# One decoder trunk, two ways to set the order of its instructions

## The chip, the cores and the metric

The kernel runs on 1 core of one Trainium2 chip. The metric is the device time of the program in microseconds; for the kernel before it is 1557.64 us, the median of 3 runs (1557.45 to 1557.89).

A core has five instruction streams that matter here: TensorE (PE, matmuls into eight PSUM banks), VectorE (DVE), ScalarE (ACT), GpSimd (POOL) and SyncE (SP), whose stream here only starts DMA transfers. Each works through its own queue in the order in which it was written, and waits on semaphores for the results of the others.

## The reference

Two decoder layers on 512 tokens of width 1024. Layer 0 mixes tokens by retention (4 heads), layer 1 by an mLSTM (4 heads); after each comes a causal ConvFFN of width 2816. Each of the four blocks is normed, modulated by columns computed from `c`, and added to the residual.

```python
c_act = silu(c)
for i in range(2):
    sh_t, sc_t, gt_t, sh_f, sc_f, gt_f = split(c_act @ ada_w[i] + ada_b[i], 6)
    h = rmsnorm(x, norm_tok_g[i]) * (1 + sc_t) + sh_t
    y = retention_mixer(h) if i == 0 else mlstm_mixer(h)
    x = x + gt_t * y
    h = rmsnorm(x, norm_ffn_g[i]) * (1 + sc_f) + sh_f
    u = causal_dwconv(h @ w_up[i], conv_w[i], conv_b[i])      # 3 taps
    a, b = split(u, 2)
    x = x + gt_f * ((silu(a) * b) @ w_down[i])
return rmsnorm(x, final_g)

# retention, per head, chunks of 128: q, k rotated by position (rope)
s = (q @ k.T) * decay;  y = groupnorm(s @ v + cross part) ;  out = (silu(g) * y) @ w_out
# mLSTM, per head: q, k through a 4-tap conv and silu; two gates give running weights
s = (q @ k.T) * w_intra;  h = (s @ v + ...) / max(|den|, exp(-m));  y = groupnorm(sigmoid(o) * h);  out = y @ w_out
```

## The kernel before, in words

**Layout and arithmetic.** Activations lie transposed, 128 channels on the partitions and 512 tokens along them; the residual `x` is eight tiles of 128x512. Products are in fp32r with both operands split into a high and a low part: `mm3` (L277 to L279) makes three matmuls, high by high, high by low, low by high. So each weight chunk of 0.5 MB (`Chunk`) is loaded into a `raw` buffer, ScalarE casts its high part (`high_part`, L160), and VectorE subtracts to get the low part (`low_part`, L165). `Pair.split` (L273, L274) does the same for activations.

**Stages.** `ret_start` norms the input and makes the first head's values and gates; then come the four retention heads (`heads`: q and k with `rope`, scores, values, gates, attend, group norm, output product), the norm into the ConvFFN (`Start`), the ConvFFN, the same for the mLSTM with its gates, the second ConvFFN, and the last norm with the stores (`End`). The recurrence over chunks is not computed step by step: each head covers all 512 tokens at once, in four strips of 128 keys.

Across a norm the work is cut in two halves of 256 tokens (`boundary`): the last output products run for half 0 and then for half 1, so that the first half's norm (squares L304 and L307, their sums L311, `root` L287 to L292, scaled tiles L328 and L331, high and low parts L337 and L339) runs beside the products of the second.

In a ConvFFN the products of most channel tiles run in a folded form (`folded`), 17 units of seven products with 256 columns (L418 to L420), two accumulating DMAs on GpSimd's queue and one of the down products per unit.

**What sets the order.** The program is a list of `items` (one or several weight chunks and a function that uses them). `Ahead` issues the load, the high part and the low part of a chunk up to four items before its use. In two places, `ret_start` and `folded.run`, the order of TensorE, VectorE, ScalarE and GpSimd is written out by hand: they stand in a `tc.manual_schedule` block, which keeps the program's order on these engines. Everywhere else the framework's own scheduler orders the instructions when the program is built, with the program's order as priority. Buffers come from pools: 55 slots of 128x512, six `raw`, eight high and eight low weight buffers, two `a` buffers, eight PSUM banks; a tile takes a free buffer of its pool.

**Modulation columns.** The columns of `c_act @ ada_w` are made one by one: a load of 0.5 MB and a VectorE multiply with accumulation (`gemv`, L140). 16 are made in `ret_start`. The other 80 wait in `side`: one or two go with each item until `LATER` = 32 are left; folded loop 0 takes eight of these (one in every second unit), and the items after it take the last 24.

The line numbers of the page are those of this kernel.

Of the kernel before, what the change touches and what calls it, by code (L numbers as in the profile page):

```python
# [29 lines left out]
LATER = 32  # L30
# [11 lines left out]
STRIPS = [(0, 512), (128, 384), (256, 256), (256, 256)]  # L42

# [25 lines left out]

@with_exitstack  # L70
def trunk(ctx: ExitStack, tc: tile.TileContext, xT, cb, pos, vec, ident, decay, zmask, ada, w_s0, w_in0, w_v0,
# [17 lines left out]

    def slot(s, dt=F32, w=T):  # L90
        return slots.tile([P, w], dt, tag="s", name=uid(s))

    def wide(s, dt=F32):
        if dt == F32:
            return raws.tile([P, D + 1], F32, tag="raw", name=s)
        return wpool.tile([P, WCOLS + WPAD], dt, tag=s[:3], name=s)

    def bank(s):
        return psum.tile([P, T], F32, tag="ps", name=uid(s))

    def aside(s):
        return asides.tile([P, D + 1], F32, tag="a", name=uid(s))

    V, A, G, PE = nc.vector, nc.scalar, nc.gpsimd, nc.tensor
# [3 lines left out]
    V.memset(const.tile([P, 32], F32, tag="pad", name="pad")[:], 0.0)  # L108
    ones = {}
    for name, v in (("d", 1.0 / D), ("v", 1.0 / DV), ("1", 1.0)):  # L110
        o = const.tile([P, P], F32R, tag=f"ones{name}", name=f"ones_{name}")
        V.memset(o[:].bitcast(F32), v)
        ones[name] = o
# [3 lines left out]
    nc.sync.dma_start(c_row[:1, :D], cb)  # L117
    x = [slot("x") for _ in range(KT)]
    for m in range(KT):
        nc.sync.dma_start(x[m][:], xT[m])  # L120
    c_ext = cond.tile([P, D + 1], F32, tag="c", name="c_ext")
    vecs = const.tile([P, NVEC], F32, tag="vec", name="vecs")
# [5 lines left out]
    eps_t = const.tile([P, 1], F32, tag="eps", name="eps_t")  # L128
    V.memset(eps_t[:], EPS)
    V.memset(const.tile([P, 40], F32, tag="pad2", name="pad2")[:], 0.0)  # L130
    V.memset(c_ext[:, D : D + 1], 1.0)

    mods = [const.tile([P, 48], F32, tag=f"mod{i}", name=f"mod_{i}") for i in range(2)]
    gains = [const.tile([P, 2 * KT], F32, tag=f"gain{i}", name=f"gain_{i}") for i in range(2)]

    def gemv(layer, f, raw=None):
        if raw is None:
            raw = aside("ada")[:]
            nc.sync.dma_start(raw, ada[layer, f])
        return V.scalar_tensor_tensor(raw, raw, 1.0, c_ext[:], op0=ALU.mult, op1=ALU.mult,  # L140
                                      accum_out=mods[layer][:, f : f + 1])

    def side_work(layer, f, after, raw=None):
        tc.keep_in_program_order(gemv(layer, f, raw))
        after()
# [22 lines left out]
    def low_part_added(w, hi, r, off=0):  # L168
# [3 lines left out]
        nc.gpsimd.dma_start(lo.bitcast(F32), w[:, r], accum_op=ALU.add)  # L172
        return lo

    class Chunk:
        def __init__(self, src, n, off):
            self.raw, self.r, self.off = wide(uid("raw")), slice(0, n), off
            nc.sync.dma_start(self.raw[:, self.r], src)
# [10 lines left out]
    class Beside(Chunk):  # L189
# [3 lines left out]
        def __init__(self, src):  # L193
            self.raw, self.r, self.off = aside("raw"), slice(0, WCOLS), 0
            nc.sync.dma_start(self.raw[:, :WCOLS], src)
# [13 lines left out]
    class Fold:  # L209
# [5 lines left out]
        def load(self):  # L215
            src = self.src
            self.a, self.b = wide(uid("wa")), wide(uid("wb"))
            nc.sync.dma_start(self.b[:, :WCOLS], src[1])
            nc.sync.dma_start(self.a[:, :WCOLS], src[0])
# [142 lines left out]
    class Ahead:  # L362


        def __init__(self):
            self.at = self.at_high = self.at_low = 0

        @property
        def flat(self):
            if not hasattr(self, "all"):  # L370
                self.all = [u for n, (uses, _, _) in enumerate(items) for u in uses if u.first == n]
            return self.all

        def may(self, n):
            u = self.flat[self.at]
            if any(n <= b < u.first for b in bars):
                return False
            return u.first <= n + AHEAD and (self.at < WBUFS or self.flat[self.at - WBUFS].last < n)

        def load(self):  # L380
            u = self.flat[self.at]
            u.chunk = Chunk(u.src, u.n, u.off)
            self.at += 1

        def high(self):
            self.flat[self.at_high].chunk.high()
            self.at_high += 1

        def low(self):
            self.flat[self.at_low].chunk.low()  # L390
            self.at_low += 1
    ahead = Ahead()

# [11 lines left out]
    def folded(folds, h, terms, pairs, downs, modulate):  # L405
# [4 lines left out]
        banks, sums, other = {}, {}, []  # L410
# [25 lines left out]
        def unit(i):  # L436
# [24 lines left out]
            else:  # L461
                ahead.high()
                ahead.high()
# [16 lines left out]
            else:  # L480
                ahead.low()
                ahead.low()
# [4 lines left out]
            if f:  # L487
                f.high_24()
                f.low_24(i % 2)
                if other:  # L490
                    layer, m, after, raw = other.pop()
                    gemv(layer, m, raw)
                    after()
            else:
                ahead.high()
                ahead.high()
# [13 lines left out]
            else:  # L510
                ahead.low()
                ahead.low()
# [5 lines left out]
            if modulate and side and i % 2 == 0 and i + 2 < len(folds):  # L518
                layer, m, after = side.pop(0)
                raw = aside("ada")[:]  # L520
                nc.sync.dma_start(raw, ada[layer, m])
                other.append((layer, m, after, raw))
            if i == len(folds) - 2:
                for _ in range(4):
                    ahead.load()
# [7 lines left out]
        def run(w):  # L533
            with tc.manual_schedule(engines={mybir.EngineType.PE, mybir.EngineType.DVE, mybir.EngineType.Activation,
                                             mybir.EngineType.Pool}):
                for i in range(len(folds)):
                    unit(i)
                last(len(folds) - 1)
                at = pairs[-1]
                c1, c2 = banks[len(folds) - 1]  # L540
                at.init(1, c2)
                at.init(0, c1)
                at.taps(1)
                at.taps(0)
                at.silu()
                at.gate()
                at.high()
                at.low()
        return first(), run

    def center_split(v, ps):

        t, m = slot("vt"), cols.tile([P, 1], F32, tag="vm", name=uid("vm"))
# [121 lines left out]
    class Start(Norm):  # L675
# [53 lines left out]
        def sums(self):  # L729
# [3 lines left out]
            d, xr = cols.tile([P, 4], F32, tag="dsh", name=uid("dsh")), self.xr  # L733
# [36 lines left out]
    class End(Norm):  # L770
# [7 lines left out]
        def use(self, p, k0, k1):  # L778
# [3 lines left out]
            for m in range(k0, k1):  # L782
# [3 lines left out]
                else:  # L786
                    tc.keep_in_program_order(
                        V.scalar_tensor_tensor(o[:, at : at + n], x[m][:, r], self.gain(m), self.rs[p][:, r],
                                               op0=ALU.mult, op1=ALU.mult))
            nc.sync.dma_start(out[k0:k1, :, r].rearrange("m p t -> p m t"),  # L790
# [120 lines left out]
    class Ffn:  # L911
# [77 lines left out]
        def items(self, norm):  # L989
# [4 lines left out]
            steps, run = folded(folds, self.h, self.start.terms, pairs, downs, self.layer == 0)  # L994
# [88 lines left out]
    def ret_scores(i):  # L1083
        st = R[i]
        tab = slot("tab")
        nc.sync.dma_start(tab[:], decay[i])
# [34 lines left out]
    def ret_start():  # L1121
# [16 lines left out]
        def load_ada(f, buf=None):  # L1138
            mod[f] = (buf or wide(uid("ada")))[:, : D + 1]
            nc.sync.dma_start(mod[f], ada[0, f])  # L1140

        def load_raw(k):
            raw[k] = wide(uid("raw"))
            nc.sync.dma_start(raw[k][:, :D], w_s0[k])
# [34 lines left out]
        with tc.manual_schedule(engines={mybir.EngineType.PE, mybir.EngineType.DVE, mybir.EngineType.Activation,  # L1179
# [386 lines left out]
```

## Time and profile before

| what | value |
|---|---|
| time, median of 3 runs | 1557.64 us |
| time of the profiled execution | 1559.0 us |
| its span, first to last instruction | 1557.2 us |
| mean granted TensorE clock | 0.993 |
| TensorE busy | 1519.7 us, 9037 matmuls |
| VectorE busy | 1194.2 us, 1832 instructions |
| ScalarE busy | 857.9 us, 1277 instructions |
| GpSimd busy | 205.4 us, 232 instructions |
| read from HBM | 193.13 MB |

A row of a group names the line, the engine, the operation, the tiles (written from read), the shape and the count, then busy us, the mean ns of one, and the idle time before them with what ended it. In a row of waits, the engine and its instruction stand before the arrow and what it waited for behind it. In a row of the timeline the first two numbers are the start and the duration in us; the bracket is the idle time ahead of it and what ended that. The end of a matmul is modelled, so matmuls overlap in the record.

### The profile page before, as it was taken

The numbers are of one execution on the slowest core, as the hardware profiler recorded it, in microseconds if no ns is written. First come the engines' busy times: TensorE is split into PE (matmuls) and PEld (weight loads), VectorE is DVE, ScalarE is ACT, GpSimd is POOL, SyncE is SP. The second block draws the span as 40 slices with busy tenths as digits, with TensorE's granted clock in tenths as the row PEclk, the third lists the DMA queues.
The fourth block names the chain that finished last, engine by engine and source line by source line (L and its number), as shares of the span: only waits on it lengthen the run. The fifth ranks groups of instructions, "written<-read, shape, count | busy, mean of one in ns | idle before, by whom it ended". The sixth has DMA issues, their size and how long they took to land.

```text
span 1557.2 us, 23255 instructions
## 1 busy us (share of the span) xinstructions
PE 1519.7 (98%) x9037; PEld 1344.6 (86%) x9037; DVE 1194.2 (77%) x1832; ACT 857.9 (55%) x1277; POOL 205.4 (13%) x232
## 2 busy tenths in 40 slices
PE   9999999999999999999999899999999999999997
PEld 7778888887988999999988778888889889999997
DVE  7985778686997888887776677776788977777775
ACT  4534524453456777676654444454545666777763
POOL 0121001110130111111100011001022201111102
PEclk9999999999999999999999999999999999999999
DMA  8833465545315888788434342443422258777751
GB/s 299 313 115 109 142 192 171 187 163 181 123 41 126 211 210 220 208 200 209 160 127 131 122 122 95 135 131 116 159 69 69 69 134 193 198 193 186 188 141 55
DMA packets 72369, 241.87 MB, mean 155 GB/s; under 512 B 9905, under 2 KB 12337, under 8 KB 72258
## 3 DMA queue, kind: packets, MB, share of 16 engines
q1 hardware_dynamic: 59874, 195.28, 37.8%
q0 software_dynamic: 12384, 45.09, 15.3%
q8 instruction: 71, 1.16, 0.3%
q14 instruction: 40, 0.33, 0.1%
HBM read 193.13 MB, written 2.12 MB: 125 GB/s over the span
## 4 chain that ended last, share of the span: by engine, by line
PE 75%; DVE 14%; issue 4%; ACT 3%; DMA 3%; POOL 1%; SPq 0%; DVEq 0%; ACTq 0%; POOLq 0%
PE p L418 7%; PE p L419 7%; PE p L420 7%; PE po L277 7%; PE po L278 7%; PE po L279 7%; PE pp L277 6%; PE pp L278 6%; PE pp L279 6%; DVE wlo L165 3%; PE pv L578 3%; PE pv L579 3%; PE pv L580 3%; DVE ada L140 2%; DVE x L591 1%
## 5 line engine op out<-in xcount | busy, mean ns | idle before, releaser
L160 ACT CAST whi<-raw 128x1024 fp32r<-128x1024 f32 (+1 forms) x189 | 193.1, 1029 | 138.1 <-PE po L278 51.4
L165 DVE TENSOR_TENSOR wlo<-raw,whi 128x1024 fp32r<-128x1024 f32 (+1 forms) x157 | 189.3, 1213 | 46.2 <-ACT whi L160 45.9
L277 PE MATMUL pp<-hh,whi 128*128 128x512 f32 x552 | 215.7, 391 | 2.8 <-ACT vt L554 2.4
L278 PE MATMUL pp<-hl,whi 128*128 128x512 f32 x552 | 215.6, 391 | 0.0
L279 PE MATMUL pp<-hh,wlo 128*128 128x512 f32 x552 | 215.4, 390 | 0.0
L591 DVE SCALAR_TENSOR_TENSOR x<-po,mod,x 128x512 f32<-128x512 f32 (+1 forms) x184 | 114.1, 630 | 71.2 <-PE po L279 67.7
L278 PE MATMUL po<-ggl,whi 128*128 128x512 f32 (+1 forms) x448 | 153.6, 344 | 0.0
L279 PE MATMUL po<-ggh,wlo 128*128 128x512 f32 (+1 forms) x448 | 153.0, 343 | 0.0
L277 PE MATMUL po<-ggh,whi 128*128 128x512 f32 (+1 forms) x448 | 152.8, 344 | 0.1
L418 PE MATMUL p<-hh,whi 128*128 128x256 f32 x544 | 150.3, 276 | 0.0
L419 PE MATMUL p<-hl,whi 128*128 128x256 f32 x544 | 150.2, 276 | 0.0
L420 PE MATMUL p<-hh,wlo 128*128 128x256 f32 x544 | 150.2, 276 | 0.0
L140 DVE SCALAR_TENSOR_TENSOR ada<-ada,c_ext 128x1025 f32<-128x1025 f32 x96 | 117.0, 1220 | 30.4 <-DMA ada<-ada 30.2
L277 PEld LDWEIGHTS pp<-hh,whi 128*128 128x128 f32 x552 | 104.0, 188 | 25.1 <-ACT vt L554 2.8
L279 PEld LDWEIGHTS pp<-hh,wlo 128*128 128x128 f32 x552 | 104.0, 188 | 21.9
L278 PEld LDWEIGHTS pp<-hl,whi 128*128 128x128 f32 x552 | 103.9, 188 | 21.3
L277 PE MATMUL po<-yh,whi 128*128 128x256 f32 (+1 forms) x352 | 115.5, 328 | 0.0
L278 PE MATMUL po<-yl,whi 128*128 128x256 f32 (+1 forms) x352 | 115.3, 328 | 0.0
L279 PE MATMUL po<-yh,wlo 128*128 128x256 f32 (+1 forms) x352 | 115.3, 327 | 0.0
L923 ACT ACTIVATE cv<-p,vecs 128x512 f32<-128x512 f32 x68 | 53.1, 781 | 96.1 <-PE p L420 57.2
L928 DVE SCALAR_TENSOR_TENSOR cv<-p,vecs,cv 128x511 f32<-128x511 f32 (+1 forms) x136 | 101.0, 745 | 2.2
L418 PEld LDWEIGHTS p<-hh,whi 128*128 128x128 f32 x544 | 102.1, 188 | 0.1
(302 smaller groups left out, 3968.0 us busy)
## 6 DMA issues: line engine op xcount, KB each, us to landing
ada<-ada SPq DMA_DIRECT2D x96, 512.5 KB, 4.4
raw<-w_in SPq DMA_DIRECT2D x61, 512.0 KB, 4.3
wb<-w_up SPq DMA_DIRECT2D x34, 512.0 KB, 4.3
wa<-w_up SPq DMA_DIRECT2D x34, 512.0 KB, 5.1
wlo<-wa POOLq DMA_DIRECT2D x34, 512.0 KB, 4.8
wlo<-ws POOLq DMA_DIRECT2D x34, 512.0 KB, 5.1
raw<-w_o SPq DMA_DIRECT2D x32, 512.0 KB, 4.2
raw<-w_dn SPq DMA_DIRECT2D x32, 512.0 KB, 4.3
```

What stands on the lines that cost most here:

```text
L140: return V.scalar_tensor_tensor(raw, raw, 1.0, c_ext[:], op0=ALU.mult, op1=ALU.mult, accum_out=mods[layer][:, f : f + 1])
L160: A.copy(hi, w[:, r])
L165: V.tensor_tensor(lo, w[:, r], hi.bitcast(F32), op=ALU.subtract)
L277: PE.matmul(o, ah, bh, start=start, stop=False)
L278: PE.matmul(o, ah, bl, start=False, stop=False)
L279: PE.matmul(o, al, bh, start=False, stop=stop)
L418: PE.matmul(o, hi[:, ch], b[0], start=st, stop=False, skip_group_check=True)
L419: PE.matmul(o, hi[:, ch], b[1], start=False, stop=False, skip_group_check=True)
L420: PE.matmul(o, lo[:, cl], b[0], start=False, stop=sp, skip_group_check=True)
L591: V.scalar_tensor_tensor(x[m][:, r], ps[:, r], gate_col, x[m][:, r], op0=ALU.mult, op1=ALU.add)
L923: A.activation(acc[:], ps[:], AF.Identity, bias=col("fcb", self.layer * 2 * FT + f), scale=self.conv_col(f, 2))
L928: V.scalar_tensor_tensor(acc[:, s:], ps[:, : T - s], self.conv_col(f, j), acc[:, s:], op0=ALU.mult, op1=ALU.add)
```

## The change

All instructions are now recorded first and issued at the end. `V`, `A`, `G`, `PE` and the new `S` (SyncE) are stand-ins: each call becomes a `Call` in `Plan.calls`, each tile a `Buf` that takes a real buffer only when its first call is issued. `note` finds which earlier calls a call depends on from the parts of tiles that both touch.

`Plan.add` gives each call a price (`occ`: how long it holds its engine) and a delay until others see it. `Plan.order` gives each call a due time: a TensorE call's is the sum of the prices of the TensorE calls before it in the program, another's is counted back from the calls that use it, or from the first user of the PSUM bank that it frees. `Plan.run` then steps through a modelled time. On each engine it takes, of the calls that could start soonest (to 0.02 us), the one that is due first, and leaves an early one aside if a more urgent one would become ready while it runs (`HURRY`). A call that needs a new buffer may not start more than `EARLY` = 30 us ahead of its due time, less what TensorE lags. DMAs are modelled as one queue at 2.45 us a MB (5.4 where they accumulate).

The order that comes out is issued as it is, inside one `manual_schedule` block that now covers SyncE too. Calls recorded between `plan.pin = uid("pin")` and `plan.pin = None` keep their order on each engine among themselves: these are the part of `ret_start` up to the last bank, and both folded loops. The loop over `k` in `ret_start`, the copies after it and the rope tables are no longer in a block with a fixed order. `Ahead` is gone: a chunk's load and both parts are recorded at the item that first uses it. `LATER` is 24 instead of 32, the folded loops make no modulation columns, and the items before loop 0 take two columns at every fifth instead of every tenth item past the 20th. A column's load has the first TensorE call of its item as a predecessor in the plan.

The core of the diff:

```diff
-LATER = 32
+LATER = 24
+KINDS = {"s": NSLOTS, "whi": WBUFS, "wlo": WBUFS, "raw": RAWS, "a": 2, "ps": 8, "vm": 4, "dsh": 4}
+HURRY = 1.5
+EARLY = 30.0
...
+class Plan:
+    LAT = dict(PE=0.23, DVE=0.18, ACT=0.18, POOL=0.2, SP=0.1)
...
+    def add(self, eng, obj, name, a, k):
...
+        if name == "dma_start":
+            size = max((v.box[1] - v.box[0]) * v.width for v, _ in views) * 4e-6
+            c.dma = size * (5.4 if "accum_op" in k else 2.45) + 0.05
+            c.occ = 0.9 if eng == "POOL" else 0.4
+        elif eng == "PE":
...
+            c.occ = max(o * 4.427e-4, 0.06) * (1 if single else 4)
+        elif eng == "DVE":
+            if name == "reciprocal":
+                c.occ = 0.05 + 6.45e-3 * width
+            elif name in ("tensor_scalar", "tensor_copy", "memset"):
+                c.occ = 0.12 + 4.5e-4 * width
+            else:
+                c.occ = 0.09 + 1.06e-3 * width + (0.1 if "accum_out" in k else 0)
+        elif eng == "ACT":
+            c.occ = 0.1 + 8.4e-4 * width + (0.2 if "accum_out" in k else 0)
...
+        else:
+            c.occ = 0.15 + 2.3e-3 * width if name == "tensor_tensor" else 0.3 + 1.7e-3 * width * (width > 1)
+        c.lat = self.LAT[eng]
...
+        for c in calls:
+            c.due = pe_time + (0.0 if c.eng == "PE" else 30.0)
+            pe_time += c.occ * (c.eng == "PE")
+        for n in range(len(calls) - 1, -1, -1):
+            c = calls[n]
+            for m, real in c.succs if c.eng != "PE" else ():
+                s = calls[m]
+                c.due = min(c.due, s.due - c.occ - (self.tail(c) if real else 0.0))
+            for b in c.bufs:
+                if b.psum and c.eng != "PE" and b.turn + 8 in users:
+                    first = calls[users[b.turn + 8][0]]
+                    c.due = min(c.due, first.due - c.occ - self.tail(c))
...
+            soonest = min(t for _, _, t in cand) + 0.02
+            for due, n, t in cand:
+                if t > soonest:
+                    continue
+                end = t + calls[n].occ
+
+                if e == "PE" or not any(d < due and t < t2 < end and d + lag - end < HURRY for d, _, t2 in cand):
+                    return t, e, n
...
+            if c.dma:
+                dma_free = max(dma_free, t + occ + 1.2) + c.dma
+                c.end = dma_free + 0.9
+            else:
+                c.end = t + occ + c.lat
...
+    def issue(self):
+        for n in self.order():
+            c = self.calls[n]
+            real = lambda v: v.get() if isinstance(v, View) else v
+            getattr(c.obj, c.name)(*[real(v) for v in c.a], **{key: real(v) for key, v in c.k.items()})
...
+    plan = Plan()
+    V, A, G, PE, S = (plan.engine(*p) for p in (("DVE", nc.vector), ("ACT", nc.scalar), ("POOL", nc.gpsimd),
+                                                ("PE", nc.tensor), ("SP", nc.sync)))
...
-    class Ahead:
...
-            if modulate and side and i % 2 == 0 and i + 2 < len(folds):
-                layer, m, after = side.pop(0)
-                raw = aside("ada")[:]
-                nc.sync.dma_start(raw, ada[layer, m])
-                other.append((layer, m, after, raw))
...
-            with tc.manual_schedule(engines={mybir.EngineType.PE, mybir.EngineType.DVE, mybir.EngineType.Activation,
-                                             mybir.EngineType.Pool}):
-                for i in range(len(folds)):
-                    unit(i)
...
+            plan.pin = uid("pin")
+            for i in range(len(folds)):
+                unit(i)
...
+            plan.pin = None
...
-        while ahead.at < len(ahead.flat) and ahead.may(n):
-            ahead.load()
-            ahead.high()
-            ahead.low()
+        gate = len(plan.calls)
+        for u in uses:
+            if u.first == n:
+                u.chunk = Chunk(u.src, u.n, u.off)
+                u.chunk.high()
+                u.chunk.low()
         fn([u.chunk for u in uses])
...
+        late = n > bars[0]
+        for _ in range((n % 2) if late else (2 if n > 20 and n % 5 == 0 else 1)):
+            if len(side) > (0 if late else LATER):
+                side_work(*side.pop(0), gate)
     assert not side
+    with tc.manual_schedule(engines={mybir.EngineType.PE, mybir.EngineType.DVE, mybir.EngineType.Activation,
+                                     mybir.EngineType.Pool, mybir.EngineType.SP}):
+        plan.issue()
```

More of the change, by code (lines that the diff above doesn't have):

```diff
@@ L1 @@
+from bisect import bisect, insort
 from contextlib import ExitStack
@@ L361, in trunk @@
     bars = []
-    class Ahead:
[L365 to L392, printed above, removed]
     side = []
```

524 lines of the change are left out of this document (350 added, 174 removed).

## The prediction

> **What bounds the kernel now.** I read the page's first two parts first. The numbers after each engine are busy us, share of the span and instructions.
>
> ```profile
> span 1557.2 us, 23255 instructions
> PE 1519.7 (98%) x9037; PEld 1344.6 (86%) x9037; DVE 1194.2 (77%) x1832; ACT 857.9 (55%) x1277; POOL 205.4 (13%) x232
> ```
>
> TensorE is the bound and is busy for 98% of the span. No matmul is removed, so everything to be had lies in 1557.2 - 1519.7 = 37.5 us of idle TensorE, plus what it loses at a lower clock. Next I cut the span where the idle time lies (columns: stretch, its length, busy us of PE, PEld, DVE, ACT, POOL, granted clock, DMA share, GB/s).
>
> ```profile
> 0.00:20.00 20.00, 18.22 (x48) 12.60 (x49) 9.01 (x26) 9.69 (x17) 0.73 (x5) 1.00 0.87 316
> 20.00:64.00 44.00, 44.00 (x193) 36.32 (x192) 41.83 (x65) 18.17 (x23) 0.00 (x0) 1.00 0.85 302
> 64.00:125.00 61.00, 55.25 (x234) 44.32 (x233) 52.79 (x81) 25.72 (x41) 13.75 (x13) 0.94 0.49 168
> 125.00:355.00 230.00, 230.00 (x1076) 193.87 (x1075) 161.57 (x227) 99.24 (x151) 28.50 (x34) 1.00 0.50 162
> 355.00:410.00 55.00, 53.44 (x298) 45.91 (x297) 43.78 (x72) 18.76 (x29) 3.21 (x4) 1.00 0.48 153
> 410.00:460.00 50.00, 47.59 (x391) 46.52 (x391) 46.33 (x80) 24.85 (x53) 15.75 (x16) 0.97 0.19 64
> 460.00:725.00 265.00, 265.00 (x1819) 244.16 (x1818) 215.08 (x342) 189.19 (x261) 35.77 (x42) 1.00 0.76 193
> 725.00:765.00 40.00, 38.83 (x316) 37.78 (x315) 28.09 (x48) 22.26 (x39) 2.99 (x4) 1.00 0.61 182
> 765.00:805.00 40.00, 36.97 (x309) 36.18 (x309) 30.69 (x48) 21.91 (x40) 9.63 (x10) 1.00 0.31 106
> 875.00:960.00 85.00, 77.08 (x359) 62.97 (x358) 60.88 (x90) 41.29 (x67) 13.98 (x16) 0.98 0.35 106
> 960.00:1195.00 235.00, 234.55 (x1187) 200.25 (x1186) 172.15 (x244) 111.58 (x164) 21.95 (x23) 1.00 0.36 115
> 1195.00:1225.00 30.00, 26.53 (x227) 25.91 (x226) 29.64 (x49) 15.82 (x35) 12.74 (x13) 1.00 0.18 54
> 1520.00:1557.00 37.00, 27.28 (x228) 26.28 (x226) 21.02 (x38) 13.11 (x30) 9.28 (x12) 0.91 0.17 58
> ```
>
> Length less PE busy gives the idle time: 1.78 us at the start, 5.75 at 64 (first retention head), 1.56 at 355, 2.41 at 410 (norm into ConvFFN 0), 1.17 at 725 (folded end), 3.03 at 765 (norm into mLSTM), 7.92 at 875 (first mLSTM heads), 0.45 at 960, 3.47 at 1195 (norm into ConvFFN 1), 9.72 at the end. The long stretches at 125 and 460 have none. The clock column adds loss while busy: 6% of 61 us, 3% of 50 and 2% of 85 is 3.7 + 1.5 + 1.7 = 6.9 us.
>
> **The change part by part.**
>
> (a) *TensorE may go on with other work.* From 64 to 125, from 355 to 410 and from 875 to 1195 there are independent projections beside the product that waits. The waits there are these (PE's own, in us, times, longest):
>
> ```profile
> PE pp L277 <- ACT vt L554: 2.4, 1, 2.4
> PE psc L277 <- ACT qkh L273: 2.2, 1, 2.2
> PE pav L277 <- ACT sh L273: 4.4, 1, 4.4
> PE pden L287 <- ACT o L1375: 1.7, 1, 1.7
> ```
>
> Each is a place where another engine took the urgent piece late. The first: ScalarE had casts of later weights queued ahead of the copy that frees a PSUM bank, and those casts stood waiting for loads.
>
> ```profile
> 63.45 1.05 ACT L160 CAST whi<-raw 128x1024 fp32r<-128x1024 f32 x1 [1.98 <-DMA raw<-w_in]
> ...
> 66.93 0.59 ACT L554 ACTIVATE vt<-pst 128x512 f32<-128x512 f32 x1
> 67.67 0.50 PE L277 MATMUL pp<-hh,whi 128*128 128x512 f32 x1 [2.37 <-ACT vt L554]
> 68.73 0.63 PE L278 MATMUL pp<-hl,whi 128*128 128x512 f32 x1
> 75.06 0.39 PE L278 MATMUL pp<-hl,whi 128*128 128x512 f32 x1
> ```
>
> The 4.4 us one: the load that head 0's mLSTM weights need is issued only when the program reaches it, and lands 4.3 us later, though its source is written once for all heads when the mLSTM's gates are done.
>
> ```profile
> 876.32 0.38 SPq L1354 DMA_DIRECT2D mb<-scratch x1
> DMA to landing us min/median/max: 4.3/4.3/4.3
> 880.67 0.35 DVE L1361 SCALAR_TENSOR_TENSOR w<-mb,bcols,zm 128x128 f32<-128x128 f32 x1 [2.92 <-DMA mb<-scratch]
> ```
>
> The new list gives each piece a due time counted back from the matmul that uses it, lets a load go out up to 30 us ahead of that, and lets TensorE take the next startable product when the due one is late. All three undo exactly these waits. Idle in these stretches is 5.75 + 1.56 + 7.92 + 0.45 = 15.7 us. With it goes half clock: after the 2.37 us gap the matmul takes 0.63 us instead of 0.39, and the clock column for the stretches at 64 and 875 gives 3.7 + 1.7 = 5.4. Together 21.1. I leave 3 of it standing: PSUM has eight banks, all full at 65, so one evacuation stays exposed. Gain 18.
>
> By the Trainium skill (TensorE: Matmul & The Clock Gate, Part 1) the clock falls to half after about 3.4 us without work. By that, only the 4.4 us gap would cost clock here, and the sum would be some 5 us smaller. The trace disagrees: 2.37 us were enough.
>
> (b) *The norm boundaries* (410, 765, 1195). Nothing but the norm feeds the next layer, so there TensorE has only the halves that the program already staggers. Idle is 2.41 + 3.03 + 3.47 = 8.9 us, clock 1.5. The waits are the split of the sum of squares and the last scaled tiles:
>
> ```profile
> PE pms L287 <- ACT ssh L273: 5.7, 3, 2.1
> PE pf L278 <- DVE hl L339: 2.9, 4, 1.3
> 436.98 1.21 DVE L165 TENSOR_TENSOR wlo<-raw,whi 128x1024 fp32r<-128x1024 f32 x1
> ...
> 438.45 0.68 DVE L239 TENSOR_TENSOR ws<-wb 128x512 f32<-128x512 f32 x1
> ...
> 439.50 0.41 ACT L273 CAST ssh<-ssq 128x256 fp32r<-128x256 f32 x1 [2.55 <-DVE ssq L311]
> ```
>
> VectorE, 46.33 of 50 us busy, takes weight splits and sums of weights between the squares' sums; ordered by due time, about 2 us leave this chain at each boundary. But VectorE itself is the bound there (29.64 of 30 us at 1195), and the list's price for its short pieces is too low where GpSimd works beside it: 0.09 + 1.06e-3 x 256 = 0.36 us each, against
>
> ```profile
> 429.76 0.47 DVE L339 SCALAR_TENSOR_TENSOR hl<-xr,mod,hh 128x256 fp32r<-128x256 f32 x1
> 445.30 4.47 DVE L339 SCALAR_TENSOR_TENSOR hl<-xr,mod,hh 128x256 fp32r<-128x256 f32 x5
> ```
>
> 0.47 us alone and 0.89 in the run of five. So I take half: bounds 0 and 10.4, taken 5. The Trainium skill (SBUF — State Buffer, SBUF: two separate sides) says that GpSimd and a VectorE operation with two SBUF inputs hold one port pair in turn, each for its whole instruction; the doubled 0.89 us agrees, and by it alone the 2.9 us of hl waits would stay.
>
> (c) *Short stalls that busy time does not show.* A 512-column matmul is recorded at 0.39 us (above), but the stream does not start one only every 0.39: in steady work twelve steps of 256 columns take 601.40 - 600.04 = 1.36 us, 0.113 each, so 512 columns 0.227.
>
> ```profile
> 600.04 0.28 PE L419 MATMUL p<-hl,whi 128*128 128x256 f32 x1
> ...
> 601.40 0.28 PE L419 MATMUL p<-t24l,whi 128*128 128x256 f32 x1
> ```
>
> So each stall hides some 0.16 us behind the modelled end of the matmul before it. The whole view of PE's waits, of which rows stand here, counts 25 of them: 25 x 0.16 = 4, of which I take 3 (bounds 0 and 4).
>
> (d) *Pinned parts.* The start up to the first products and both folded ConvFFN loops keep their order on every engine; their idle (1.78 and 1.17 us) and the tail (9.72 us: root, reciprocal, scaling, store, with no matmul left) are counted unchanged. Freed after the start's preamble, the k loop had no PE idle (20 to 64: 44.00 of 44.00), so at 0.
>
> (e) *Moved modulation columns.* LATER goes from 32 to 24, and eight loads of 0.5 MB with their VectorE products leave folded loop 0 for the retention layer. A product is 1.22 us:
>
> ```profile
> L140 DVE SCALAR_TENSOR_TENSOR ada<-ada,c_ext 128x1025 f32<-128x1025 f32 x96 | 117.0, 1220 | 30.4 <-DMA ada<-ada 30.2
> ```
>
> 8 x 1.22 = 9.8 us, in stretches where VectorE has 230 - 161.57 = 68 us free at 125 to 355 and DMA is at half. Hidden; uncovered it would cost 9.8. Folded loop 0 had no idle before 725 to gain from their leaving.
>
> (f) *New waits.* All SP loads now stand in one written order, and each of the five queues is fixed by planned times. A piece whose input comes later than planned holds what is behind it: on ScalarE a cast holds evacuations, which hold PSUM banks, which hold TensorE, as at 63.45 above. The plan lets a 0.5 MB load land 0.4 + 1.2 + 1.34 + 0.9 = 3.8 us after its issue and spaces loads by 1.34 us (393 GB/s). The trace has 4.3 to 5.1 us and, at a DMA share of 0.87, 316 GB/s:
>
> ```profile
> raw<-w_in SPq DMA_DIRECT2D x61, 512.0 KB, 4.3
> wa<-w_up SPq DMA_DIRECT2D x34, 512.0 KB, 5.1
> ```
>
> So loads come 0.5 to 1.3 us late against plan. Most are issued well before their use and nothing shows; bounds are 0 and 44 us (below, rival 3). I take 3, since the other prices of the list (1.18 us against 1.21 for a weight's low part, 0.96 against 1.05 for its cast) sit close to the rows above.
>
> The sum against the profiled execution (1559.0 us, of which 1557.2 span and 1.8 around it): 1559.0 - 18 - 5 - 3 + 3 = 1536. The median of the runs, 1557.64, lies 1.4 lower, so 1534.6; I say **1535**.
>
> **The rivals.**
>
> 1. *Only the heads' gaps close.* At the boundaries VectorE stays the bound and its pieces beside GpSimd run at 0.89 us; the late loads cost 8. For it: 29.64 of 30 us. Against it: the weight splits between the sums can go earlier. Then 1559.0 - 18 - 0 - 2 + 8 - 1.4 = 1545.6, say 1546, from 1543 to 1554.
> 2. *The order barely changes.* The list takes the due product unless its own model sees TensorE idle; where the model does not know the delay, the old order and gap stay, as it would not know the 3.43 us of this small piece on GpSimd, priced at 0.3:
>
> ```profile
> 67.71 3.43 POOL L555 TENSOR_SCALAR vm<-vm 128x1 f32<-128x1 f32 x1 [66.45 <-ACT vt L554]
> ```
>
> Against it: the delays of (a) are queue order, which any model sees. What comes back is under 3 us: 1555 to 1560.
> 3. *Slower, through late loads at the head of fixed queues.* Place: the two folded loops, 17 units each, DMA share 0.76 at 460 to 725. A unit is 265/17 = 15.6 us and brings in three loads and two accumulating ones. If one of them per unit stands 1.3 us late at the head of ScalarE's or VectorE's queue, with no slack left on TensorE, 34 x 1.3 = 44 us come in: 1559 - 23 + 44 - 1.4 = 1579. It decides from 0.7 us a unit (24 us), and ends between 1562 and 1590. Against it: weights are fetched two units ahead, and this order is kept from before, where these loops do not stall.
> 4. *Nearly all closes*, boundaries included, and hidden stalls too: 21.1 + 10.4 + 4 = 35 less: 1559 - 35 - 1.4 = 1522, from 1517 to 1527.
>
> **How the numbers follow.** Forecast (1527 to 1543) 0.48, rival 1 0.20, rival 2 0.07, rival 3 0.15, rival 4 0.10. Faster by over 0.2%, about what a measurement of this kernel can tell from no change (below 1554.5), is the forecast with rivals 1 and 4: 0.78. Rival 2 is the same: 0.07. Slower is rival 3: 0.15. The range 1518 to 1560 leaves out rival 3 and the lowest edge of rival 4. The likeliest case's own range is 1527 to 1543.
>
> **What would show it.** Right for (a): PE's waits for vt, qkh, sh and o gone, the mb load issued well before its use, the granted clock at 1.00 in the first head and in the first mLSTM heads, idle there under 4 us in sum. For (b): waits of pms and pf down to some 4 us, with VectorE still full at the boundaries. For (d) and (e): start, folded loops and tail as long as before. For (f): no new PE wait on a DMA or on whi in the folded loops. The prediction is wrong if PE busy time plus idle at the boundaries does not shrink, or if TensorE stands idle where it had none (125 to 355, 460 to 725).

## The result, and the profile after

The kernel after takes 1522.15 us, the median of 4 runs (1521.79 to 1523.57), against 1557.55 us (1555.95 to 1557.89) for the kernel before: a ratio of 0.9776, 95% interval 0.9759 to 0.9793, so 35 us less. The profiled execution took 1523.57 us with a span of 1521.7.

The page of the kernel after, its first lines, and the shares of the chain that ended last. All instructions now bear line 367, the one that issues them, so they are told apart by their tiles.

```profile
span 1521.7 us, 23272 instructions
PE 1505.3 (99%) x9037; PEld 1340.7 (88%) x9037; DVE 1198.3 (79%) x1832; ACT 865.1 (57%) x1286; POOL 218.8 (14%) x232
...
PE 95%; DVE 3%; DMA 1%; issue 1%; ACT 0%; POOL 0%; SPq 0%; DVEq 0%; POOLq 0%; ACTq 0%
```

The same chain of the kernel before, where VectorE had 14% of it, and time in which an engine waited for nothing that the profile shows (issue) 4%:

```profile
PE 75%; DVE 14%; issue 4%; ACT 3%; DMA 3%; POOL 1%; SPq 0%; DVEq 0%; ACTq 0%; POOLq 0%
```

The matmuls are the same 9037. Idle TensorE fell from 37.5 to 1521.7 - 1505.3 = 16.4 us, and its busy time by 14.4 us, because time at half clock (granted clock 0.5) and the short stalls hidden behind modelled ends count as busy. So the stretches below are cut at equal work: each begins where TensorE had done as many columns as at the border of the prediction's stretch (20, 64, 125, ... us before). Columns as there.

```profile
0.00:21.00 21.00, 17.70 (x48) 12.52 (x49) 8.70 (x25) 9.45 (x16) 0.73 (x5) 1.00 0.89 327
...
64.60:115.20 50.60, 50.60 (x235) 42.46 (x234) 46.54 (x72) 21.90 (x37) 11.64 (x13) 1.00 0.27 96
115.20:345.30 230.10, 230.10 (x1077) 194.01 (x1076) 177.59 (x249) 98.07 (x151) 38.24 (x34) 1.00 0.53 183
345.30:397.60 52.30, 52.30 (x297) 46.06 (x296) 44.48 (x66) 21.16 (x31) 4.17 (x3) 1.00 0.50 182
397.60:444.60 47.00, 46.52 (x392) 45.94 (x391) 44.77 (x82) 26.50 (x56) 14.83 (x16) 1.00 0.34 118
444.60:710.10 265.50, 265.00 (x1819) 244.02 (x1818) 211.82 (x336) 187.42 (x257) 35.48 (x42) 1.00 0.71 179
710.10:747.70 37.60, 37.60 (x317) 36.94 (x316) 27.18 (x46) 22.38 (x39) 3.18 (x4) 1.00 0.63 181
747.70:785.50 37.80, 36.29 (x310) 35.80 (x309) 30.89 (x48) 22.17 (x40) 10.30 (x10) 1.00 0.23 71
...
855.60:928.60 73.00, 73.00 (x358) 62.47 (x357) 57.51 (x79) 36.24 (x55) 14.32 (x11) 1.00 0.44 155
928.60:1162.20 233.60, 233.60 (x1186) 200.31 (x1185) 172.78 (x244) 113.81 (x168) 26.94 (x25) 1.00 0.33 115
1162.20:1189.40 27.20, 26.75 (x227) 26.34 (x227) 26.28 (x45) 14.41 (x30) 9.83 (x12) 1.00 0.29 98
...
1484.90:1521.70 36.80, 26.97 (x228) 26.16 (x226) 20.46 (x37) 12.47 (x29) 9.22 (x12) 0.93 0.17 58
```

| stretch | before, us | after, us | gained |
|---|---|---|---|
| heads: 64, 355, 875, 960 | 61 + 55 + 85 + 235 | 50.6 + 52.3 + 73.0 + 233.6 | 26.5 |
| norm boundaries: 410, 765, 1195 | 50 + 40 + 30 | 47.0 + 37.8 + 27.2 | 8.0 |
| end of folded loop 0: 725 | 40 | 37.6 | 2.4 |
| all else | 961.2 | 962.6 | -1.4 |

The heads have no idle left and the clock is at 1.00 in every stretch but the last. TensorE's whole list of waits after:

```profile
PE pc L367 <- DMA c_row<-cb: 2.0, 1, 2.0
PE pf L367 <- DVE hl L367: 1.9, 3, 1.1
PE pst L367 <- POOL warm L367: 1.3, 1, 1.3
PE p L367 <- DMA wlo<-ws: 0.8, 2, 0.5
PE pms L367 <- DVE ssl L367: 0.4, 1, 0.4
PE pms L367 <- ACT sq L367: 0.4, 1, 0.4
```

The waits for vt, qkh, sh and o are gone; all those of pms (sums of squares at a norm) and pf (first products behind it) together fell from 9.5 us to 2.7. New is pc, which waits 2.0 us in the start. At the first bank, two of ScalarE's early casts still wait for their loads, but they are done before the product ends, and the copy then goes at once (timeline of ScalarE):

```profile
61.36 1.05 ACT L367 CAST whi<-raw 128x1024 fp32r<-128x1024 f32 x1 [1.60 <-DMA raw<-w_in]
62.62 1.05 ACT L367 CAST whi<-raw 128x1024 fp32r<-128x1024 f32 x1 [0.20 <-DMA raw<-w_in]
64.60 0.60 ACT L367 ACTIVATE vt<-pst 128x512 f32<-128x512 f32 x1 [0.93 <-PE pst L367]
```

The mLSTM rows' load (view of the tile mb) goes out at 812.0 us, 14.5 us ahead of its first use at 826.5, where before it was 876.3 and 880.7:

```profile
L367 SPq DMA_DIRECT2D mb<-scratch x4: 327/352/565, 812.0 to 1085.7; - x4
DMA to landing us min/median/max: 6.3/6.3/6.3
```

### The profile page after: what moved, and what is told of

Same layout as the page of the kernel before. It is cut to its first block, busy times and chain, and to the rows that moved or that the text cites. A ratio compares the mean times of both kernels' runs of the same rounds, so it can differ in the third digit from the quotient of the medians.

```text
span 1521.7 us, 23272 instructions
## 1 busy us (share of the span) xinstructions
PE 1505.3 (99%) x9037; PEld 1340.7 (88%) x9037; DVE 1198.3 (79%) x1832; ACT 865.1 (57%) x1286; POOL 218.8 (14%) x232
## 3 DMA queue, kind: packets, MB, share of 16 engines
q0 software_dynamic: 12384, 45.09, 16.4%
## 4 chain that ended last, share of the span: by engine, by line
PE 95%; DVE 3%; DMA 1%; issue 1%; ACT 0%; POOL 0%; SPq 0%; DVEq 0%; POOLq 0%; ACTq 0%
PE po L367 26%; PE pp L367 25%; PE p L367 20%; PE pv L367 10%; PE pav L367 4%; PE pf L367 3%; PE pst L367 3%; PE psc L367 2%; DMA wlo<-ws 1%; PE pc L367 1%; DVE xr L367 1%; PE pms L367 1%; DVE hl L367 1%; DVE rs L367 0%; DVE wlo L367 0%
## 5 line engine op out<-in xcount | busy, mean ns | idle before, releaser
L367 DVE TENSOR_TENSOR wlo<-raw,whi 128x1024 fp32r<-128x1024 f32 (+2 forms) x229 | 246.3, 1091 | 63.4 <-ACT whi L367 63.0
L367 ACT CAST whi<-raw 128x1024 fp32r<-128x1024 f32 (+1 forms) x197 | 200.8, 1029 | 63.8 <-PE po L367 25.9
L367 PE MATMUL p<-hh,whi 128*128 128x256 f32 (+1 forms) x546 | 150.4, 276 | 0.0
L367 PEld LDWEIGHTS p<-hh,wlo 128*128 128x128 f32 x544 | 102.1, 188 | 1.2 <-DMA wlo<-ws 1.2
```

The source lines that it names most:

```text
L367: getattr(c.obj, c.name)(*[real(v) for v in c.a], **{key: real(v) for key, v in c.k.items()})
```

## The experiments

Each changes one thing in the kernel after or in the kernel before. Times are medians; ratios are to the kernel before in the same comparison, with 95% intervals. The name in brackets is the run's. The question behind most of them: the gain came, but through which part of the new order?

**TensorE held to the program's order (pe_program).**

```diff
+            if c.eng == "PE":
+                p = last_pin.get("PE")
+                if p is not None:
+                    c.preds.add(-1 - p)
+                last_pin["PE"] = n
```

> The kernel after, with one edge more in the plan: TensorE's calls stay in the order in which the program recorded them; the other four queues are ordered as before by due time. Service theory (the gain comes from the other engines and the loads bringing each input in time, TensorE needs no other order): 1520 to 1526 us, no new TensorE wait. Run-ahead theory (the gain of step (a) comes from TensorE taking another product while one waits): the waits for rope, mLSTM weights and denominators return, 10 us or more, 1532 or above.

Measured: 1540.05 us (1538.82 to 1542.51), ratio 0.9891 (0.9876 to 0.9906). By the number the run-ahead theory had it, but not by the place. The waits of the heads did not return; cut at equal work, the stretches from 64 to 410 and from 875 to 1195 are as long as in the kernel after, to 0.1 us. What came back lies at the end of the two folded loops, where the stretches are 7.6 and 7.4 us longer, half clock included:

```profile
PE po L372 <- ACT ggh L372: 7.6, 2, 3.8
PE p L372 <- DVE p L372: 2.0, 2, 1.0
```

There the last down products wait for the last unit's activations, and the kernel after runs other groups' down products between. The kernel before did that too: 2 us of po products stand ahead of the last p products, from 740.62 to 742.57. So TensorE's run-ahead is needed, but only there, and it is not where the gain over the kernel before comes from.

**The mLSTM rows' load held back in the plan (mb_late).**

```diff
-        S.dma_start(mb[:], scratch[i : i + 1].broadcast_to([P, T]))
+        late = [n for n, c in enumerate(plan.calls) if c.eng == "PE"][-12]
+        S.dma_start(mb[:], scratch[i : i + 1].broadcast_to([P, T])).after = late
```

> The kernel after, with the load of the mLSTM weight rows (mb, db) held in the plan until twelve matmuls before the scores of its head, as late as the program of before issued it. TensorE stays free to take other products. Run-ahead theory: hidden, within 2 us of 1522. Service theory: for each head whose attend follows its scores closely the load's 4.3 us show again, about 4.4 us plus half clock 1.7 for head 0 and less for the other three: 1526 to 1532.

Measured: 1522.77 us (1522.06 to 1523.22), ratio 0.9778 (0.9763 to 0.9792). It tells nothing on either theory: the load went out at 819.7 us and its rows were first used at 847.2, so it was not late. The hold acts in the plan's time alone: it sets the load's place in SyncE's queue, and on the chip that queue ran far enough ahead of TensorE.

**The same load issued early in the kernel before (before_mb).**

```diff
         def then(ps):
+            if "rows" not in M[i]:
+                mb, db = M[i]["rows"] = slot("mb"), slot("db")
+                nc.sync.dma_start(mb[:], scratch[i : i + 1].broadcast_to([P, T]))
+                nc.sync.dma_start(db[:], scratch[4 + i : 5 + i].broadcast_to([P, T]))
```

> The kernel before, with the load of the mLSTM weight rows issued when the first q tile of the head is done instead of at the head's scores. Nothing else changes. If the 4.4 us wait of the attend products at 879 us is that late load: 1557.6 - 4.4 - 1.7 (half clock) = 1551.5, from 1550 to 1553.5. If the wait is as much the ScalarE chain behind it (table load, exponentials, casts): at most 2 us less, 1555.5 to 1557.

Measured: 1552.31 us (1550.27 to 1556.28), ratio 0.9971 (0.9956 to 0.9985). Inside the expected range of the late-load reading, but in part by luck. The wait went from 4.4 to 1.4 us, but part of it moved into the same head's group norm (1.2 before) and, since the framework's scheduler ordered everything anew, to the first head's rope (2.2 before). Cut at equal work, the stretch at 875 is 3.4 us shorter, not 4.4 + 1.7: 3.4 us at half clock are still there, at 918 us instead of 884. Another 1.9 us came off the stretch at 725 and 1.0 off that at 355, which the run did not aim at. TensorE's waits at the places named:

```profile
PE psc L277 <- ACT qkh L273: 3.9, 1, 3.9
PE pvar L287 <- DVE vl L274: 2.4, 1, 2.4
PE pav L277 <- ACT sh L273: 1.4, 1, 1.4
```

**The first bank's copy placed ahead of the third cast, in the kernel before (before_vt).**

```diff
-            for _ in range(3):
+            for _ in range(2):
                 ahead.high()
                 ahead.low()
+            center_split(R[0]["v"], pss[0])
+            ahead.high()
+            ahead.low()
```

> The kernel before, with the first copy out of PSUM after the start (vt, and its split) placed ahead of the third weight cast in the order written by hand. Nothing else changes. If TensorE's 2.37 us wait at 65 us is ScalarE's queue order: most of it goes and the half clock behind it, 1557.6 - 1.6 - 1.7 = 1554.3, from 1553 to 1555.5. If the bank would come late anyway, because GpSimd's 3.43 us piece holds ScalarE: 1557 to 1560.

Measured: 1562.25 us (1559.93 to 1563.82), ratio 1.003 (1.0018 to 1.0041): slower, and for a reason that neither theory had. The first copy was early, and then the free order behind the block put seven casts ahead of the second (ScalarE's timeline, then TensorE's waits):

```profile
64.20 5.78 ACT L160 CAST whi<-raw 128x1024 fp32r<-128x1024 f32 x6
70.18 1.05 ACT L160 CAST whi<-raw 128x1024 fp32r<-128x1024 f32 x1 [0.20 <-DMA raw<-w_v]
71.13 0.59 ACT L554 ACTIVATE vt<-pst 128x512 f32<-128x512 f32 x1
```

```profile
PE psc L277 <- ACT qkh L273: 5.2, 1, 5.2
PE pp L277 <- ACT vt L554: 3.7, 2, 2.3
```

The wait moved one bank on, and the rope behind it became later. It was queue order, as the prediction said, but not one that a local edit mends.

**Due times by the program's order, not counted back (program_due).**

```diff
-            c.due = pe_time + (0.0 if c.eng == "PE" else 30.0)
+            c.due = pe_time
...
-            for m, real in c.succs if c.eng != "PE" else ():
+            for m, real in ():
```

(The due time from the next user of a PSUM bank is left out as well.)

> The kernel after, with the due times no longer counted back from TensorE: a call is due at TensorE's position in the program where it is recorded, as a plain program-order priority. Prices, model of buffers and loads and the fixed queues stay. If ordering by when TensorE needs a result carries the gain: the copies that free banks and the norm chains fall behind weight parts again, 1535 to 1555. If it is enough that a list with these prices fills idle engines in program order: 1520 to 1528.

Measured: 1534.18 us (1531.36 to 1535.27), ratio 0.9846 (0.9831 to 0.9862), between the two. The heads stay free of waits but for one of 1.1 us. The stretch behind the norm into ConvFFN 0 (460 to 725 before) is 275.5 us instead of 265.5, cut at equal work. There, low parts of weights come late (three of the four waits below, 5.4 us), and 6.8 us at half clock follow the last of them. That is not what the first theory had, by which copies and norm chains would fall behind the weight parts:

```profile
PE pp L367 <- DVE wlo L367: 6.5, 4, 2.3
```

So counting back is worth about 12 us, nearly all at one place, and is not what freed the heads.

**Loads that the plan takes to be instant (loads_free).**

```diff
-            c.dma = size * (5.4 if "accum_op" in k else 2.45) + 0.05
+            c.dma = 0.01
...
-                dma_free = max(dma_free, t + occ + 1.2) + c.dma
-                c.end = dma_free + 0.9
+                c.end = t + occ + c.lat
```

> The kernel after, with a plan that takes every load to land at once (no transfer time, no landing delay), so that each load comes about 4 us later than planned. Rival 3 of the prediction (late loads at the head of fixed queues cost TensorE time): stalls in the folded loops and at heads, 1540 to 1580. If loads go out so far ahead that their price hardly matters: 1520 to 1530.

Measured: 1535.02 us (1534.49 to 1536.15), ratio 0.9855 (0.9842 to 0.9869). It lies between the two ranges. A plan in which loads take no time costs 13 us, not 44: cut at equal work, 2.8 in the start, 0.9 in the first heads, 0.8 at 410, 4.4 in folded loop 0 and 2.0 in the second. On the chip the loads need not come late by that much: the mLSTM rows' load still went out at 821.4 us, 14.7 ahead of its first use. The units do not pay one by one; the waits are few:

```profile
PE p L366 <- DMA wlo<-ws: 2.3, 2, 2.0
PE pms L366 <- DVE diag L366: 2.2, 1, 2.2
```

**EARLY at 8 us (early8).**

```diff
-EARLY = 30.0
+EARLY = 8.0
```

> The kernel after, with EARLY at 8 us instead of 30: a call that needs a new buffer may start at most 8 us ahead of its due time. If the long lead is what keeps late loads harmless: some loads and splits come late, 1527 to 1545. If the due times alone are enough: 1520 to 1525.

Measured: 1538.1 us (1537.34 to 1539.41), ratio 0.9875 (0.9861 to 0.9889), within the long-lead theory's range, but not by late loads: TensorE has no new wait on one. EARLY limits the lead in the plan's time; on the chip the mLSTM rows' load went out at 822.2 us and was first used at 854.8, so its lead was not shorter. The stretch at 410 is 5.4 us longer and folded loop 0 is 3.4 longer. At the norm, modulation products and low parts now stand between its pieces (VectorE's timeline, then TensorE's wait):

```profile
417.44 1.22 DVE L367 SCALAR_TENSOR_TENSOR ada<-ada,c_ext 128x1025 f32<-128x1025 f32 x1
...
420.65 2.87 DVE L367 TENSOR_TENSOR wlo<-raw,whi 128x1024 fp32r<-128x1024 f32 x2
423.45 0.94 DVE L367 SCALAR_TENSOR_TENSOR hl<-xr,mod,hh 128x256 fp32r<-128x256 f32 x1
```

```profile
PE pf L367 <- DVE hl L367: 4.8, 3, 2.8
```

The end is 6.5 us longer. The first half's root and reciprocal, which ran at 1498 us beside the last products in the kernel after, now run behind all products, together with the second half's (VectorE's timelines, kernel after and this run):

```profile
1498.45 1.75 DVE L367 RECIPROCAL rs<-rs 128x256 f32<-128x256 f32 x1 [0.39 <-ACT rs L367]
```

```profile
1521.98 3.36 DVE L367 RECIPROCAL rs<-rs 128x256 f32<-128x256 f32 x2 [3.07 <-ACT rs L367]
```

In the last norm these pieces serve stores alone, and a store, which has no user, is due 30 us after TensorE's position; with a lead of 8 us a piece that needs a new buffer must wait until its due time is that near. That this is the reason was not tried by itself.

**VectorE, ScalarE and GpSimd 30% too cheap (cheap).**

```diff
+        if eng in ("DVE", "ACT", "POOL") and not c.dma:
+            c.occ *= 0.7
```

> The kernel after, with VectorE's, ScalarE's and GpSimd's prices cut by 30% (loads and TensorE unchanged). If the calibrated prices carry what the heads gain: the list again puts weight parts ahead of urgent pieces and the waits of the heads return, 1532 to 1550. If any list that fills idle engines does it: 1520 to 1527, with loss only where VectorE is full, at the norms.

Measured: 1545.33 us (1545.16 to 1545.56), ratio 0.9919 (0.9902 to 0.9935). The number is that of the theory by which prices carry the heads; the place is not. The heads are nearly as free as in the kernel after (50.9 us at 64, 50.6 there). Most of the loss, 17 of 23 us, is at the three norms, as the other theory said, only larger:

```profile
PE pms L369 <- ACT ssh L369: 11.2, 4, 3.1
PE pms L369 <- DVE ssl L369: 2.5, 3, 0.9
```

**TensorE 15 us late in the plan (pe_15).**

```diff
         free = dict.fromkeys(engines, 0.0)
+        free["PE"] = 15.0
```

> The kernel after, with a plan in which TensorE is busy for the first 15 us, about what it loses on the chip in the start. In the kernel after the plan lets TensorE run some 15 us earlier than it can, so that all else stands that much ahead of need. If this lead is what keeps wrong prices harmless: it goes, waits on loads and splits appear, 1526 to 1540. If the plan is right enough without it: 1519 to 1525.

Measured: 1525.3 us (1524.93 to 1526.57), ratio 0.9791 (0.9777 to 0.9806). It lies between the two ranges. The 3 us lie in the start: 67.6 us to the first head instead of 64.6; waits behind it are those of the kernel after. That the other engines' lead is not needed does not follow, because they kept it: a piece may start EARLY ahead of its due time plus what TensorE lags, so their limit moved by the same 15 us, and on the chip the mLSTM rows' load still went out 14.3 us ahead of its first use (14.5 in the kernel after).

**The folded loops without pins (unpinned).**

```diff
-            plan.pin = uid("pin")
             for i in range(len(folds)):
                 unit(i)
```

> The kernel after without the pins in the two folded loops: their calls are ordered by due time like all others. If the order written by hand there is only a safeguard: 1520 to 1525, no new TensorE wait. If the list loses there because it knows nothing of what slows the units' accumulating loads: waits of p on wlo or on VectorE's sums return in the units, 1527 to 1560.

Measured: 1522.03 us (1521.3 to 1522.67), ratio 0.9769 (0.9754 to 0.9783): the same time. The wait of p on wlo (0.8 us) is gone. The list orders the units as well as the hand did.

**No tile scaled on GpSimd at the norms (pooled_none).**

```diff
-POOLED = (1, 3, 5, 7)
+POOLED = ()
```

> The kernel after, with POOLED empty: at the norms GpSimd scales no tile, VectorE scales all eight from the residual itself, and ScalarE's copies for GpSimd fall away. If VectorE's pieces take 0.9 us there because GpSimd works beside it: they fall to 0.4 us, VectorE needs 16 x 0.4 = 6.4 us for a half's tiles instead of 8.7, and the time falls by 1 to 4 us, 1518 to 1521. If VectorE is simply out of time there: 4 x 0.4 us more at each of three boundaries and the end, 1524 to 1529.

Measured: 1521.13 us (1520.74 to 1522.37), ratio 0.9767 (0.9753 to 0.978). In the kernel after, VectorE's short pieces still double while GpSimd scales its own tiles (VectorE's and GpSimd's timelines):

```profile
428.24 2.82 DVE L367 SCALAR_TENSOR_TENSOR xr<-x,gain,rs 128x256 f32<-128x256 f32 x3
...
432.74 4.29 DVE L367 SCALAR_TENSOR_TENSOR hl<-xr,mod,hh 128x256 fp32r<-128x256 f32 x7
```

```profile
428.29 3.37 POOL L367 TENSOR_TENSOR xr<-xg,rs 128x256 f32<-128x256 f32 x4 [11.26 <-DVE rs L367]
```

That is 0.94 us for one xr. Without GpSimd's four, later xr pieces take 0.54 and hl pieces 0.42, though VectorE has four more of them:

```profile
432.50 2.15 DVE L367 SCALAR_TENSOR_TENSOR xr<-x,gain,rs 128x256 f32<-128x256 f32 x4
434.57 1.67 DVE L367 SCALAR_TENSOR_TENSOR hl<-xr,mod,hh 128x256 fp32r<-128x256 f32 x4
```

TensorE's wait for hl (1.9 us) is gone, and the three boundaries are 46.0, 36.4 and 26.4 us instead of 47.0, 37.8 and 27.2, so 3.2 less in the profiles. The time is 0.1 above the range of the theory that it bears out by place. The medians differ by 1.0 us and the intervals overlap: the fastest version found, but not told apart from the kernel after by time.

**AHEAD 0 in the kernel before (before_ahead0).**

```diff
-AHEAD = 4
+AHEAD = 0
```

> The kernel before with AHEAD 0 instead of 4: a weight chunk's load, cast and low part are recorded at the item that first uses the chunk, as in the kernel after, and so rank behind the urgent pieces of the items before it; the framework's scheduler still sets the order. Every variant of the new list kept the heads free of waits. If that comes from the weight parts' rank in the recorded program: the heads' waits (65, 102, 361, 879 to 953 us) mostly go, 1530 to 1545. If it comes from the framework's picture of time, in which weight parts are ready and the urgent pieces not yet: the waits stay where they are or move, 1552 to 1575.

Measured: 1566.52 us (1565.38 to 1567.41), ratio 1.0059 (1.0043 to 1.0076). Most of the heads' waits stay or grow; only those at 361 us go, and the stretch at 355 is then as short as in the kernel after:

```profile
PE pav L277 <- ACT sh L273: 4.4, 1, 4.4
PE psc L277 <- ACT qkh L273: 4.0, 1, 4.0
PE pp L277 <- DVE vl L274: 3.2, 1, 3.2
```

The weight parts' rank in the recorded program, the same now as in the kernel after, is not the cause. How the framework's scheduler judges when a piece is ready was not tested; it is one of the explanations that are left.

## Why the prediction was right, and where it was off

The direction and the range from 1518 to 1560 held; the likeliest case's own range, 1527 to 1543, did not. The forecast was 1535, the time is 1522: rival 4 (1522, at a chance of 0.10) gave the number, because nearly all of the idle time in the heads and at the boundaries closed. That its sum is met to the microsecond is luck: it had 25 us for the heads with all hidden stalls and 10.4 for the boundaries, where 26.5 and 8.0 were gained, with 2.4 more at 725 and 1.4 lost elsewhere.

- **Step (a), the heads.** The largest term and the most mis-sized: 18 us, with 3 for hidden stalls in (c), against 26.5 measured. Two things failed in it. The 3 us "left standing" for banks did not stand: ScalarE's copy at 64.60 follows its product at once. And hidden stalls were counted only where PE's waits list one; the stretches at equal work show about 5 us more than idle and half clock together (15.7 + 5.4 = 21.1). Counted from one start of a matmul to the next, against the steady 0.113 us for 256 columns, these stretches lose 8.0 us besides idle time and clock in the kernel before and 2.2 in the kernel after; the twelve waits listed there, at 0.16 us each, make only 2.
- **Its mechanism** was half right. It named three causes: due times counted back, loads up to 30 us early, TensorE taking other products. At the two places that were touched in the kernel before, when a piece goes out is the cause: before_mb took 3 us off the wait it aimed at, before_vt moved the wait by moving the casts. Two of the three causes are not needed, each taken out alone: with TensorE in program order the heads lost nothing, with due times not counted back 1.5 us of their 26.5. Early loads stay open: in mb_late, early8, loads_free and pe_15 the mLSTM rows' load still went out 14 us or more ahead on the chip, and before_mb shows that such a lead is worth something by itself. Prices 30% too low cost the heads under 1 us. What every variant shares is the list itself, in which a piece goes when its engine is free in a modelled time; but also the fixed order of SyncE's loads, the moved columns and the freed k loop, and none of these was put into the kernel before by itself. Which of them the order of the framework's scheduler lacks is not settled; the weights' rank (before_ahead0) is ruled out. The rule by which a short piece waits for a more urgent one (HURRY) was not tried alone.
- **Step (b), the boundaries.** 5 predicted, 8.0 measured (bound 10.4). The pms waits went, as argued; GpSimd's doubling of VectorE's pieces stayed, as argued, but cost less than the 5.4 us allowed for it: without it (pooled_none) these stretches are 3.2 us shorter in the profile. Here prices do carry: cheap lost 23 us, 17 of them in these three stretches.
- **Step (d), pinned parts.** Taken at 0, and 2.4 us were gained at 725. The step took a pinned order to mean unchanged idle time, but when a load lands is not pinned. In the kernel before a p product waits there for its accumulating load:

```profile
PE p L420 <- DMA wlo<-wt: 1.0, 1, 1.0
```

That load was issued at 727.55 us and landed 9.0 later. In the kernel after it is issued at the same place in the unit, lands 6.3 us later, and nothing waits for it. This is 1.1 us of the 2.4 us; another 0.4 is a wait of p on VectorE that is gone too, and the rest is spread thin. Why the load lands sooner was not tried. The start, which was to stay as long, is 0.6 us longer (64.6 instead of 64.0 us to the first head).

- **Step (e), moved columns.** Hidden, as said: VectorE's busy time from 115 to 345 rose from 161.57 to 177.59 us, and TensorE is busy for all 230.10.
- **Step (f), late loads.** 3 us were taken; start, long stretches, folded loops and end together are some 1.4 us longer. The sign set for it, no new wait on a load in the folded loops, is met nearly: p waits 0.8 us for wlo<-ws, where it waited 1.0 for wlo<-wt. Rival 3 falls with that; even a plan that takes loads to be instant lost 13 us and not 44.
- **Rival 1** had the right reason (VectorE beside GpSimd, shown by pooled_none) and the wrong size. **Rival 2** falls.
- **The clock.** The forecast that half clock goes with gaps of 2.4 us is borne out: with the gaps gone, all stretches but the last show 1.00. The length of a gap does not decide alone: in the kernel before the 2.0 us wait of pms at 440 us was followed by half clock, and the one of 2.1 us behind the norm at 1195 was not.

## What to carry to other kernels

When the bound engine is 98% busy, cut the span where its idle time lies, compare stretches at equal work rather than busy time, and expect half clock and short stalls to come on top of the idle time shown (14.4 of the 35.5 us here). Closing one gap in a queue that a scheduler orders freely moved the wait elsewhere (before_vt); one list with prices close to the chip's closed them together. Where the engines have slack, rough prices do; where one is full, at the norms here, prices 30% too low cost 17 of the 35 us gained. And a delay put into a plan is not a delay on the chip (mb_late, early8, pe_15): read from the trace whether the change did what it was meant to do.

## What had not been expected

- ScalarE loads its function tables more often in the list's order, 42 times instead of 33; none of TensorE's waits names it:

```profile
L367 ACT ACT_TABLE_LOAD x42 | 53.9, 1283 | 18.4 <-DVE mc L367 7.6 <-DVE grs L367 4.3 <-DMA mb<-scratch 2.2
```

- GpSimd's first small piece, 3.43 us in the kernel before, took 1.25 in the kernel after, and in before_vt it was the second that took 7.30. The runs do not show what sets it.
